# Rotary stage of a four-branch decoder trunk taken from PSUM with scaled tables, and a step per tile at the start of the last branch

## The chip, the cores and the metric

The program runs on one core of one Trainium2 chip. Its time is the device time of one execution in microseconds (us). Five engines run their own in-order queues: TensorE (PE, matmuls), VectorE (DVE), ScalarE (ACT), GpSimd (POOL) and SyncE (SP, which here issues DMAs). Matmul results land in PSUM, in banks of 128 x 512 float32 numbers, and are read from there by DVE or ACT.

## What is computed

The reference is a decoder trunk of two layers, 512 tokens, width 1024, in float32. Each layer runs four causal token mixers over one shared input projection, gates and adds them, and then a SwiGLU:

```python
for l in range(DEPTH):                       # DEPTH = 2
    h = rms_norm(x, ln1[l])
    u = h @ w_in
    fq, fk, fv, ff, gq, gk, gv, glr, gr, rq, rk, rv, rg, z, xbc, dt, gates = split_cols(u, IN_SPLITS)
    y_a = forgetting_attention(fq, fk, fv, ff + fox_bf, fox_qn, fox_kn)   # per-head RMS norm of q and k first
    o_b = gla_chunked(gq, gk, gv, log_a)
    o_c = retention_chunked(apply_rotary(rq, cos, sin), apply_rotary(rk, cos, sin), rv, log_gamma)
    o_d = ssd_chunked(...)
    merged = sum of sigmoid(gate_b) * (y_b @ w_up_b) over the four branches
    x = x + merged @ w_out
    x = x + swiglu(rms_norm(x, ln2[l]), w_ffn_in, w_ffn_out)

def apply_rotary(x, cos, sin):
    x1, x2 = x[..., :half], x[..., half:]    # half = 32 of a head's 64 channels
    return concatenate([x1 * cos - x2 * sin, x1 * sin + x2 * cos], axis=-1)
```

## The kernel before

Activations lie with the channels on the partitions and the 512 tokens along the free axis, so a tile of 128 x 512 holds two heads of 64 channels. Each float32 operand is split into a high and a low part in a reduced float32 type (`split` at L213 to L216: an ACT cast for the high part, a DVE subtraction for the low part), and a product is made as three matmuls, high by high, high by low and low by high (`mm3`), or as two (`mm2`) where one side is an exact constant.

**Weights** are streamed in slabs of 128 x 1024 (eight blocks of 128 x 128). For each slab SP issues a DMA into `wr`, ACT casts it to `wh` (L214), and DVE subtracts to `wl` (L215), two slabs ahead of their use.

**A projection tile** (`proj`) is eight k-blocks of three matmuls, 24 matmuls of 128 x 512 into one bank of the pool `mm` (four banks). Then a DVE instruction takes it out: L487 multiplies it with the norm's root `n1.r`, L1157 does the same for a gate tile, and L1171 multiplies the output of an up-projection (6 matmuls for a branch of 256 channels) with its gate. All else uses four banks of a second pool, `mx`. A bank is written again four tiles later, and not before the instruction that takes its old contents out.

**Order.** The four mixers are Python generators: `ssd`, `gla`, `ret` (retention) and `fox` (the forgetting attention). `drain(gen, PACE[i])` runs one to its next `yield w` and then emits projection and up-projection tiles from the list `fill` worth w times PACE[i] us (5.2 us for each projection tile); what is overdrawn is carried over. The scheduler of the framework then fixes the order on each engine at build time; at run time each engine takes its instructions strictly in that order.

**Names and lines that matter here.** `gate_quad` (L1148 on) makes a tile `g` of four gate tiles and applies one ACT sigmoid of 128 x 2048 when the fourth is there. ACT functions belong to sets of tables: Ln and Exp to one, Sigmoid to another, and `act` (L233, L238) issues an ACT_TABLE_LOAD where the set changes. In `ret()`, four tiles rq and rk (two each) are split, multiplied with the constant `perm` (L923, two matmuls of 128 x 512 for each tile, which exchange the halves of 32 channels with a sign), and put together as rq*cosT + (perm rq)*sinT by a DVE, a POOL and a DVE instruction (L928 to L930). In `fox()`, the four tiles fq and fk are normed: their squares are split and summed per head on PE with the constant `bones` (the bank named `mx`, from `t` and `cr`), ACT takes Ln and Exp of each (1/root), `newton` refines it with three DVE instructions (L371 reads the bank, L372, L373), and DVE L1036 scales the tile. Up to this change all of that comes before one `yield 2`, and `stack(0, 0)` before a `yield` of 1.

Of the kernel before, what the change touches and what calls it, by code (L numbers as in the profile page):

```python
# [13 lines left out]
AF = mybir.ActivationFunctionType  # L14
ALU = mybir.AluOpType
# [3 lines left out]
P = 128  # L19
S = 512  # L20
D = 1024
KD = D // P
# [10 lines left out]
C_RQ, C_RK, C_RV, C_RG = 1812, 2068, 2324, 2580  # L33
# [4 lines left out]
WARM = 11  # L38
TILE = 5.2
LAG = 1  # L40
PACE = (4.5, 5.0, 5.0, 7.5)
WIDE = 256 + 28
PARTS = (6, 6, 6, 4)
PLAIN = 2
# [11 lines left out]
def _const_parts():  # L56
    i = np.arange(P)
    same = (i[:, None] // 64) == (i[None, :] // 64)
    up = (i[:, None] <= i[None, :]).astype(np.float64)
    perm = np.zeros((P, P))  # L60
    for m in range(P):
        if m % 64 < 32:
            perm[m + 32, m] = -1.0
        else:
            perm[m - 32, m] = 1.0
    dret = np.zeros((P, NH, P))
    rel = i[None, :] - i[:, None]
    for h in range(NH):
        dret[:, h, :] = np.where(rel >= 0, np.exp(np.maximum(rel, 0) * LOGG[h]), 0.0) * 0.125
    qdec = np.zeros((P, 2, P))  # L70
    for j in range(2):
        for half in range(2):
            qdec[64 * half:64 * half + 64, j, :] = np.exp((i + 1.0) * LOGG[2 * j + half])[None, :]
    kdec = np.exp((P - 1.0 - i)[:, None] * LOGG[None, :]) * 0.125
    inv = (10000.0 ** (-np.arange(32) / 32.0))[i % 32][:, None]
    sgn = np.repeat(np.array([-1.0] * 4 + [1.0] * 8)[None, :], P, 0)
    one = np.ones((P, 1))
    exact = [
        ("uo", np.concatenate([up, np.ones((P, P))], 1)),
        ("lst", (i[:, None] > i[None, :]).astype(np.float64)),  # L80
        ("bones", same.astype(np.float64)),
        ("ubd", up * same),
        ("perm", perm),
        ("sel8", ((i[:, None] % 8 == np.arange(8)[None]) & (i[:, None] < 64)).astype(np.float64)),
        ("selc", ((i[:, None] % 32 // 4 == np.arange(8)[None]) & (i[:, None] < 64)).astype(np.float64)),
        ("sel4", ((i[:, None] % 4 == np.arange(4)[None]) & (i[:, None] % 32 < 16) & (i[:, None] < 64)).astype(np.float64)),
    ]
    return exact, [
        ("ident", np.eye(P)),
        ("dret", dret.reshape(P, -1)),  # L90
        ("qdec", qdec.reshape(P, -1)),
        ("kdec", kdec),
        ("inv", inv),
        ("sgn", sgn),
        ("blk8", (i[:, None] // 8 == np.arange(4)[None]).astype(np.float64)),
        ("blkc", np.where(i < 64, 1.0, -1.0)[:, None] * (i[:, None] % 4 == np.arange(4)[None])),
        ("blk4", (i[:, None] // 4 == np.arange(4)[None]).astype(np.float64)),
        ("eps", one * EPS),
        ("one", one),
        ("hpi", one * (math.pi / 2)),  # L100
    ]
# [33 lines left out]
def trunk(ctx: ExitStack, tc: tile.TileContext, keys, qkeys, xin, pos, wst, wsq, par, ext, cst, out):  # L135
    nc = tc.nc
    V, A, G, T = nc.vector, nc.scalar, nc.gpsimd, nc.tensor

    cp = ctx.enter_context(tc.tile_pool(name="cp", bufs=1))
    gap = [ctx.enter_context(tc.tile_pool(name="gap0", bufs=1))]  # L140
# [22 lines left out]

    def phase(**bufs):
        if not pools:
            for g, n in zip(gap, (32, 256)):
                if n:
                    pad(g, n)
        st = ExitStack()
        pad(st.enter_context(tc.tile_pool(name=nm("gap"), bufs=1)), 128 if "fp" in bufs else 64)  # L170
        for n, b in bufs.items():
            pools[n] = st.enter_context(tc.tile_pool(name=nm(n), bufs=b, reuse_waits="tile"))
        return st
# [4 lines left out]
    def TT(dtype=F32):  # L178
        return pools["tp"].tile([P, S], dtype, tag="t", name=nm("t"))

    def NT(dtype=F32):
        return np_.tile([P, S], dtype, tag="n", name=nm("n"))
# [7 lines left out]
    def MX():  # L190
        return px.tile([P, S], F32, tag="mx", name=nm("mx"))
# [16 lines left out]
    def mm2(o, l, r, start, stop):  # L208
        pairs = [(a, r) for a in l] if isinstance(l, tuple) else [(l, b) for b in r]
        for i, (a, b) in enumerate(pairs):  # L210
            mm(o, a, b, start and i == 0, stop and i == 1)
# [6 lines left out]
    def split_tile(t):  # L218
        return split(t, TT(F32R), TT(F32R))
# [9 lines left out]
    def act(out, in_, func, **kw):  # L229
        want = {AF.Ln: "natural_log_exp_and_others", AF.Exp: "natural_log_exp_and_others", AF.Silu: "silu_and_others", AF.Sin: "silu_and_others", AF.Sigmoid: "sigmoid_and_others"}.get(func)  # L230
        pre = None
        if want and want != seen["set"]:
            pre = A.preload_act_table_set(want)  # L233
            if seen["last"] is not None:
                order(pre, seen["last"])
            seen["set"] = want
            seen["pre"] = pre
        i = A.activation(out=out, in_=in_, func=func, **kw)  # L238
        if want:
            order(i, seen["pre"])  # L240
            seen["last"] = i
        return i
# [90 lines left out]
    def C(n):  # L333
        o, w = CONST_OFF[n]
        return cs[:, o:o + w]

    def R(n):
        o, w = EXACT_OFF[n]
        return cr[:, o:o + w]

    ident = C("ident")
    lst, bones, ubd, perm, uo = (R(n) for n in ("lst", "bones", "ubd", "perm", "uo"))
    sel8 = R("sel8").rearrange("p (g r) -> p r g", g=2)
    sel4, selc = R("sel4"), R("selc")
    U, ones = uo[:, :P], uo[:, P:2 * P]
# [6 lines left out]
    cosT = cp.tile([P, S], F32, name="cosT")  # L352
    sinT = cp.tile([P, S], F32, name="sinT")

    def rotary():
        ang = TT()
        V.tensor_copy(out=ang, in_=posi.pop())
        V.tensor_scalar(out=ang, in0=ang, scalar1=C("inv"), scalar2=None, op0=ALU.mult)
        n = TT()
        V.tensor_scalar(out=n, in0=ang, scalar1=1.0 / (2 * math.pi), scalar2=12582912.0, op0=ALU.mult, op1=ALU.add)  # L360
        V.tensor_scalar(out=n, in0=n, scalar1=-12582912.0, scalar2=None, op0=ALU.add)
        for c in _two_pi_parts():
            V.scalar_tensor_tensor(out=ang, in0=n, scalar=-c, in1=ang, op0=ALU.mult, op1=ALU.add)
        V.tensor_scalar(out=ang, in0=ang, scalar1=3.1415925, scalar2=-3.1415925, op0=ALU.min, op1=ALU.max)
        act(out=sinT, in_=ang, func=AF.Sin)
        act(out=n, in_=ang, func=AF.Abs)
        act(out=cosT, in_=n, func=AF.Sin, scale=-1.0, bias=hpi)

# [66 lines left out]
    def proj(name, l, c, src, nk):  # L435
        ps = MM()
        for k in range(nk):
            mm3(ps, block(name, l, k, c), src[k], k == 0, k == nk - 1)
        return ps

    def layer(l, n1, scope):
# [9 lines left out]
        fill = []  # L451
# [32 lines left out]
        def scaled(ps, scale=None):  # L484
            t = TT()
            if scale is None:
                V.tensor_tensor(out=t, in0=ps, in1=n1.r, op=ALU.mult)  # L487
            else:
                V.scalar_tensor_tensor(out=t, in0=ps, scalar=scale, in1=n1.r, op0=ALU.mult, op1=ALU.mult)
            return t  # L490
# [18 lines left out]
        def keep(dst, i, c, scale=None):  # L509
            def go():  # L510
                dst[i] = scaled(proj("w_in", l, c, n1, KD), scale)
            return TILE, go

        def tokmajor(dst, c, stacked=False):
# [77 lines left out]
        ps = MX()  # L592
# [321 lines left out]
        rq, rk, rv = [None] * 2, [None] * 2, []  # L914
        yc = [None] * 2

        def ret():
            pp = []
            sr = [split_tile(t) for t in rq + rk]
            yield 0.8  # L920
            for t in sr:
                ps = MX()
                mm2(ps, perm, t, True, True)  # L923
                pp.append(ps)
            yield
            for ps, t in zip(pp, rq + rk):
                u = TT()
                V.tensor_tensor(out=u, in0=ps, in1=sinT, op=ALU.mult)  # L928
                G.tensor_tensor(out=t, in0=t, in1=cosT, op=ALU.mult)
                V.tensor_tensor(out=t, in0=t, in1=u, op=ALU.add)  # L930
            yield
            qd = []
            for j in range(2):
                t = TT()
# [3 lines left out]
            for j in range(2):  # L938
# [6 lines left out]
                for half, ps in enumerate(pa):  # L945
                    t = TT()
# [4 lines left out]
            for j in range(2):  # L951
                ps = MX()
                for tb in range(NB):
                    T.transpose(ps[:, tb * P:(tb + 1) * P], rk[j][:, tb * P:(tb + 1) * P], ident)  # L954
                t = TT()
# [3 lines left out]
            ps = MX()  # L959
# [55 lines left out]
        def fox():  # L1015
# [8 lines left out]
            for q in fsq:  # L1024
                ps = MX()
# [3 lines left out]
            for ps in pn:  # L1029
                u = TT()  # L1030
                act(out=u, in_=ps, func=AF.Ln, scale=1.0 / 64, bias=eps)
                rs_.append(u)
            for i, u in enumerate(rs_):
                act(out=u, in_=u, func=AF.Exp, scale=-0.5)
                newton(u, pn[i], 64)
                V.scalar_tensor_tensor(out=qk[i], in0=qk[i], scalar=g8 if i < 2 else PR("fkn"), in1=u, op0=ALU.mult, op1=ALU.mult)  # L1036
            yield 2

            stk = {}

# [59 lines left out]
                    ya[hd // 2] = split_tile(t)  # L1100

            stack(0, 0)
            yield
            pend = []
            t = None
            step = 0
# [77 lines left out]

        fill += [keep(gq, j, C_GQ + P * j, 0.125) for j in range(2)] + [keep(gk, j, C_GK + P * j) for j in range(2)]
        fill += silus([C_GR, C_GR + P, C_RG, C_RG + P])
        fill += [keep(rq, j, C_RQ + P * j) for j in range(2)] + [keep(rk, j, C_RK + P * j) for j in range(2)]
        drain(ssd(), PACE[0])
        fill += tokmajor(rv, C_RV)
        fill += gate_quad(3, 0) + mix(gate_quad(3, 1), up_of(3, 0))  # L1190
# [17 lines left out]
        m = merged  # L1208
# [323 lines left out]
```

## Time and profile before

| | before |
|---|---|
| median of 3 runs | 1709.49 us (1709.37 to 1709.84) |
| the profiled execution's own time | 1709.5 us |
| its span in the profile | 1707.8 us |
| busy: DVE, ACT, POOL | 1215.3 us (71%), 863.5 us (51%), 216.8 us (13%) |

The span runs from the first to the last instruction that the profiler recorded; 1.7 us of the execution lie around it. The busy time of an engine is the sum over its instructions. Matmuls are pipelined: each one of 128 x 512 lasts 0.39 to 0.40 us in the records, while the next one begins about 0.23 us after it.

### The profile page before, as it was taken

To read this page: it belongs to the slowest core of one execution; us is meant where nothing else is said; L and a number is where in the kernel's file an instruction comes from. 1 tells how busy PE (TensorE), PEld (TensorE's weight loads), DVE (VectorE), ACT (ScalarE), POOL (GpSimd) and SP (SyncE) were. 2 spreads that over 40 slices of the span, in tenths; PEclk is the share of its full clock that TensorE was granted. 3 is DMA by queue.
4 is the path that set the end of the run, shared out by engine and by line. 5 is a ranking of instruction groups with operands and counts; after the bars stand their busy time and mean duration, and the time that the engine had idled before them with its cause. 6 is when DMAs were issued, how large, how long until landed. Compare 5 with 4: busy or idle time off the path is not lost.

```text
span 1707.8 us, 25188 instructions
## 1 busy us (share of the span) xinstructions
PE 1695.8 (99%) x10164; PEld 1475.3 (86%) x10164; DVE 1215.3 (71%) x1691; ACT 863.5 (51%) x1190; POOL 216.8 (13%) x221
## 2 busy tenths in 40 slices
PE   8999999999999999999999999999999999999998
PEld 7878888888888999998988788888888889999997
DVE  6867676768677677676777666767776677767666
ACT  5435543546347646464544354435554474655643
POOL 3021220022101010101020212201221010101010
PEclk9999999999999999999999999999999999999999
DMA  5322222222235657575333222222222365665753
GB/s 206 100 74 75 75 87 75 87 87 74 88 110 141 193 133 188 136 184 120 92 100 111 73 75 75 90 81 89 76 85 87 99 177 160 152 176 139 186 105 105
DMA packets 54693, 195.00 MB, mean 114 GB/s; under 512 B 6064, under 2 KB 6448, under 8 KB 54576
## 3 DMA queue, kind: packets, MB, share of 16 engines
q1 hardware_dynamic: 45072, 160.45, 29.9%
q0 software_dynamic: 8640, 31.46, 10.4%
q8 instruction: 79, 1.29, 0.3%
q10 hardware_dynamic: 864, 1.48, 0.2%
q14 instruction: 38, 0.31, 0.1%
HBM read 191.28 MB, written 2.10 MB: 113 GB/s over the span
## 4 chain that ended last, share of the span: by engine, by line
PE 96%; DVE 1%; ACT 1%; DMA 1%; issue 0%; ACTq 0%; DVEq 0%
PE mm L200 65%; PE mx L200 31%; PE mx L1082 1%; DMA x<-in_x_dram 0%; DMA t<-in_ext_dram 0%; ACT wh L214 0%; DVE wl L215 0%; PE mx L692 0%; DVE t L372 0%; ACT L233 0%; DVE t L836 0%; ACT g L238 0%; DVE t L1171 0%; PE mx L954 0%; PE mx L871 0%
## 5 line engine op out<-in xcount | busy, mean ns | idle before, releaser
L214 ACT CAST wh<-wr 128x1024 fp32r<-128x1024 f32 (+1 forms) x240 | 250.1, 1043 | 359.8 <-PE mm L200 207.5
L200 PE MATMUL mm<-xh,wh 128*128 128x512 f32 (+1 forms) x1184 | 428.4, 362 | 1.4 <-DVE t L1171 0.9
L200 PE MATMUL mm<-xh,wl 128*128 128x512 f32 (+1 forms) x1184 | 427.5, 361 | 0.0
L200 PE MATMUL mm<-xl,wh 128*128 128x512 f32 (+1 forms) x1184 | 427.5, 361 | 0.0
L215 DVE TENSOR_TENSOR wl<-wr,wh 128x1024 fp32r<-128x1024 f32 (+1 forms) x220 | 285.6, 1300 | 110.3 <-ACT wh L214 108.0
L200 PEld LDWEIGHTS mm<-xh,wh 128*128 128x128 f32 x1184 | 222.4, 188 | 36.3 <-DVE t L1171 1.8
L200 PEld LDWEIGHTS mm<-xl,wh 128*128 128x128 f32 x1184 | 222.4, 188 | 34.4 <-issue 1.5
L200 PEld LDWEIGHTS mm<-xh,wl 128*128 128x128 f32 x1184 | 222.5, 188 | 33.8 <-issue 0.6
L200 PE MATMUL mm<-t,wh 128*128 128x512 f32 x448 | 140.3, 392 | 0.0
L200 PE MATMUL mx<-xh,wh 128*128 128x256 f32 (+1 forms) x448 | 136.1, 311 | 3.1 <-ACT wh L214 3.1
L200 PE MATMUL mx<-xl,wh 128*128 128x256 f32 (+1 forms) x448 | 138.3, 309 | 0.0
L1290 POOL DMA_DIRECT2D wl<-in_wsq_dram x60 | 52.0, 867 | 517.4 <-ACT wl L1289 416.4
L200 PE MATMUL mx<-f,wh 128*128 128x512 f32 x352 | 108.2, 390 | 0.0
L200 PE MATMUL mm<-f,wh 128*128 128x512 f32 x352 | 105.9, 389 | 0.0
L200 PEld LDWEIGHTS mm<-t,wh 128*128 128x128 f32 x448 | 83.2, 188 | 17.3
L215 DVE TENSOR_TENSOR l<-rq,wh 128x1024 fp32r<-128x1024 f32 x60 | 73.2, 1220 | 33.0 <-ACT wh L214 18.6
L200 PEld LDWEIGHTS mx<-xh,wh 128*128 128x128 f32 x448 | 84.0, 188 | 9.3 <-ACT wh L214 4.2
L200 PE MATMUL mx<-xh,wl 128*128 128x256 f32 (+1 forms) x288 | 91.0, 327 | 0.0
L200 PEld LDWEIGHTS mx<-xl,wh 128*128 128x128 f32 x448 | 84.1, 188 | 5.1
L200 PE MATMUL mm<-t,wl 128*128 128x512 f32 x224 | 87.4, 390 | 0.0
L214 ACT CAST wh<-rq 128x1024 fp32r<-128x1024 f32 x60 | 63.0, 1049 | 43.8 <-PE mm L200 21.5
L200 PEld LDWEIGHTS mm<-f,wh 128*128 128x128 f32 x352 | 66.1, 188 | 13.5
(275 smaller groups left out, 3428.6 us busy)
## 6 DMA issues: line engine op xcount, KB each, us to landing
wr<-in_wst_dram SPq DMA_DIRECT2D x216, 512.0 KB, 3.5
rq<-in_wsq_dram SPq DMA_DIRECT2D x60, 512.0 KB, 5.6
wl<-in_wsq_dram POOLq DMA_DIRECT2D x60, 512.0 KB, 6.8
wr<-in_wsq_dram SPq DMA_DIRECT2D x20, 512.0 KB, 6.8
out_dram<-x SPq DMA_DIRECT2D x8, 256.0 KB, 2.0
x<-in_x_dram SPq DMA_DIRECT2D x3, 512.0 KB, 6.7
wr<-in_wst_dram SPq DMA_DIRECT2D x4, 256.0 KB, 5.6
x<-in_x_dram SPq DMA_DIRECT2D x2, 256.0 KB, 4.5
```

The costliest lines, as they stand in the source:

```text
L200: T.matmul(o, lhsT=l, rhs=r, start=start, stop=stop, skip_group_check=True)
L214: A.copy(out=hi, in_=src)
L215: V.tensor_tensor(out=lo, in0=src, in1=hi.bitcast(F32), op=ALU.subtract)
L1082: T.transpose(ps[:, W:W + P], zs[qb][:, kb * P:(kb + 1) * P], ident)
L1290: G.dma_start(out=lo, in_=wsq[j], accum_op=ALU.add)
```

## The change

The rotary stage no longer goes through PE. `turned` takes the place of `keep` for the four tiles rq and rk: when their projection is in its bank, four ACT copies of 32 partitions each write the halves exchanged into `u`, DVE multiplies the bank with cosT times the norm's root, `u` with sinT times the norm's root, and adds. The two tables are made once in each layer, and the sign is put into sinT (a per-partition factor of the Sin activation). The first three parts of `ret()` go, with their yields (0.8 + 1 + 1), and PACE[2] goes from 5.0 to 7.0, so that the remaining yields of `ret` ask for as much `fill` as before (49 us). In `fox()` the `yield 2` behind the norm becomes a `yield 0.4` behind each of its four tiles, and the `yield` behind the first `stack` becomes `yield 1.4`: 3.0 in both. The first padding of memory goes from 32 to 0, which with the constant `perm` gone moves the tiles behind the constants by 512 bytes.

```diff
-PACE = (4.5, 5.0, 5.0, 7.5)
+PACE = (4.5, 5.0, 7.0, 7.5)
...
-        ("perm", perm),
...
+        ("turn", np.where(i % 64 < 32, -1.0, 1.0)[:, None]),
...
-            for g, n in zip(gap, (32, 256)):
+            for g, n in zip(gap, (0, 256)):
...
-        act(out=sinT, in_=ang, func=AF.Sin)
+        act(out=sinT, in_=ang, func=AF.Sin, scale=C("turn"))
...
+        tables = []
+
+        def turned(dst, i, c):
+            def go():
+                if not tables:
+                    for e in (cosT, sinT):
+                        tables.append(NT())
+                        V.tensor_tensor(out=tables[-1], in0=e, in1=n1.r, op=ALU.mult)
+                ps = proj("w_in", l, c, n1, KD)
+                t, u = TT(), TT()
+                for a in range(0, P, 32):
+                    A.copy(out=u[a:a + 32], in_=ps[a ^ 32:(a ^ 32) + 32])
+                V.tensor_tensor(out=t, in0=ps, in1=tables[0], op=ALU.mult)
+                V.tensor_tensor(out=u, in0=u, in1=tables[1], op=ALU.mult)
+                V.tensor_tensor(out=t, in0=t, in1=u, op=ALU.add)
+                dst[i] = t
+            return TILE, go
...
         def ret():
-            pp = []
-            sr = [split_tile(t) for t in rq + rk]
-            yield 0.8
-            for t in sr:
-                ps = MX()
-                mm2(ps, perm, t, True, True)
-                pp.append(ps)
-            yield
-            for ps, t in zip(pp, rq + rk):
-                u = TT()
-                V.tensor_tensor(out=u, in0=ps, in1=sinT, op=ALU.mult)
-                G.tensor_tensor(out=t, in0=t, in1=cosT, op=ALU.mult)
-                V.tensor_tensor(out=t, in0=t, in1=u, op=ALU.add)
-            yield
...
                 V.scalar_tensor_tensor(out=qk[i], in0=qk[i], scalar=g8 if i < 2 else PR("fkn"), in1=u, op0=ALU.mult, op1=ALU.mult)
-            yield 2
+                yield 0.4
...
             stack(0, 0)
-            yield
+            yield 1.4
...
-        fill += [keep(rq, j, C_RQ + P * j) for j in range(2)] + [keep(rk, j, C_RK + P * j) for j in range(2)]
+        fill += [turned(rq, j, C_RQ + P * j) for j in range(2)] + [turned(rk, j, C_RK + P * j) for j in range(2)]
```

Over both layers PE loses 16 matmuls of 128 x 512 and keeps all others; DVE loses 8 each of L215 (128 x 512), L487, L928 and L930 and gains 28 (4 tables, 24 in `turned`); ACT loses 8 casts and gains 32 copies of 32 x 512; POOL loses the 8 of L929; SP issues the same DMAs in the same order. ACT's table loads keep their number.

**ACT at the norm of fox, first layer.** Before, with `t_2815`, `t_2817`, `t_2819` and `t_2821` the roots of the four tiles, `mx_...` the banks with their sums, `g_2611` a tile of four gates and `wh_...` the casts of slabs:

```order
L238 ACTIVATE t_2815<-mx_2803,cs 128x512
L238 ACTIVATE t_2817<-mx_2806,cs 128x512
L238 ACTIVATE t_2815<-t_2815 128x512
L238 ACTIVATE t_2817<-t_2817 128x512
L238 ACTIVATE t_2819<-mx_2809,cs 128x512
L238 ACTIVATE t_2819<-t_2819 128x512
L238 ACTIVATE t_2821<-mx_2812,cs 128x512
L238 ACTIVATE t_2821<-t_2821 128x512
L233 ACT_TABLE_LOAD
L238 ACTIVATE g_2611<-g_2611 128x2048
L214 CAST wh_3000<-wr_2998 128x1024
L233 ACT_TABLE_LOAD
```

And with the change (the four roots are `t_2802`, `t_2804`, `t_2806` and `t_2808`, the gates `g_2604`; the line numbers are those of the changed file, L232 for L238, L227 for L233 and L208 for L214):

```order
L232 ACTIVATE t_2802<-mx_2790,cs 128x512
L232 ACTIVATE t_2804<-mx_2793,cs 128x512
L232 ACTIVATE t_2802<-t_2802 128x512
L232 ACTIVATE t_2804<-t_2804 128x512
L227 ACT_TABLE_LOAD
L232 ACTIVATE g_2604<-g_2604 128x2048
L227 ACT_TABLE_LOAD
L232 ACTIVATE t_2806<-mx_2796,cs 128x512
L208 CAST wh_2988<-wr_2986 128x1024
L232 ACTIVATE t_2808<-mx_2799,cs 128x512
L232 ACTIVATE t_2806<-t_2806 128x512
L232 ACTIVATE t_2808<-t_2808 128x512
```

The first two roots are unchanged; the load of the sigmoid's tables, the sigmoid and the load back now stand ahead of the third and the fourth root, and so does the cast `wh_2988`, which stood behind the sigmoid before.

**DVE at the same place.** Before, with L371 to L373 the steps of `newton`, L1171 (from `mm_2847` and `mm_2902`) and L1157 (from `mm_2918`) the instructions that take banks of projections out:

```order
L371 SCALAR_TENSOR_TENSOR t_2836<-mx_2809,t_2819 128x512
L372 SCALAR_TENSOR_TENSOR t_2824<-t_2824,t_2815 128x512
L372 SCALAR_TENSOR_TENSOR t_2830<-t_2830,t_2817 128x512
L371 SCALAR_TENSOR_TENSOR t_2842<-mx_2812,t_2821 128x512
L1171 TENSOR_TENSOR t_2866<-mm_2847,g_1901 128x512
L1171 TENSOR_TENSOR t_2915<-mm_2902,g_1901 128x512
L372 SCALAR_TENSOR_TENSOR t_2836<-t_2836,t_2819 128x512
L373 SCALAR_TENSOR_TENSOR t_2815<-t_2824,t_2815 128x512
L373 SCALAR_TENSOR_TENSOR t_2817<-t_2830,t_2817 128x512
L372 SCALAR_TENSOR_TENSOR t_2842<-t_2842,t_2821 128x512
L1157 TENSOR_TENSOR g_2917<-mm_2918,n_323 128x512
L215 TENSOR_TENSOR wl_3001<-wr_2998,wh_3000 128x1024
```

With the change (L365 to L367 for `newton`, L1034 for L1036, L1169 for L1171, L1155 for L1157, L209 for the subtraction that makes `wl`, L1043 and L1019 small steps of `stack` and of the next layer's constant):

```order
L209 TENSOR_TENSOR wl_2989<-wr_2986,wh_2988 128x1024
L1034 SCALAR_TENSOR_TENSOR t_2303<-t_2303,g_2788,t_2802 128x512
L365 SCALAR_TENSOR_TENSOR t_2879<-mx_2796,t_2806 128x512
L1034 SCALAR_TENSOR_TENSOR t_2336<-t_2336,g_2788,t_2804 128x512
L365 SCALAR_TENSOR_TENSOR t_2885<-mx_2799,t_2808 128x512
L1169 TENSOR_TENSOR t_2903<-mm_2890,g_1932 128x512
L209 TENSOR_TENSOR wl_3040<-wr_3037,wh_3039 128x1024
L366 SCALAR_TENSOR_TENSOR t_2879<-t_2879,t_2806 128x512
L1043 TENSOR_TENSOR t_2905<-t_2303,t_2905 64x512
L1019 TENSOR_SCALAR g_10747<-pr 128x1
L366 SCALAR_TENSOR_TENSOR t_2885<-t_2885,t_2808 128x512
L1155 TENSOR_TENSOR g_2918<-mm_2919,n_322 128x512
```

Of the two L1171 of the first listing, the counterpart of the first (it takes `mm_2816` out) now stands above these rows, behind a single L365. That of the second (`mm_2890`) stands behind `wl_2989`, which needs the cast `wh_2988`, and behind the L365 of the last two roots. The instruction that takes `mm_2919` out stands further down, behind a second slab `wl_3040`.

**ACT where rq and rk are projected, first layer.** Before, behind the Silu group of `ssd` (`t_1253` was its last):

```order
L233 ACT_TABLE_LOAD
L214 CAST wh_1428<-wr_1426 128x1024
L238 ACTIVATE t_1368<-t_1074 128x512
L238 ACTIVATE t_1370<-t_1075 128x512
L214 CAST t_1373<-t_1368 128x512
L238 ACTIVATE t_1377<-t_1076 128x512
L238 ACTIVATE t_1379<-t_1077 128x512
L214 CAST wh_1514<-wr_1512 128x1024
```

With the change:

```order
L227 ACT_TABLE_LOAD
L519 COPY t_1314<-mm_1282 32x512 x4
L208 CAST wh_1452<-wr_1450 128x1024
L519 COPY t_1377<-mm_1345 32x512 x4
L232 ACTIVATE t_1385<-t_1073 128x512
L232 ACTIVATE t_1387<-t_1074 128x512
L208 CAST t_1390<-t_1385 128x512
L208 CAST wh_1545<-wr_1543 128x1024
```

Four copies stand where each of the four tiles comes out of its bank (two of the four are seen here), between the casts of slabs and the chain of `ssd`'s norm, whose order among themselves is kept.

More of the change, by code (lines that the diff above doesn't have):

```diff
@@ L59, in _const_parts @@
     up = (i[:, None] <= i[None, :]).astype(np.float64)
[L60 to L65, printed above, removed]
     dret = np.zeros((P, NH, P))
@@ L341, in trunk @@
     ident = C("ident")
-    lst, bones, ubd, perm, uo = (R(n) for n in ("lst", "bones", "ubd", "perm", "uo"))
+    lst, bones, ubd, uo = (R(n) for n in ("lst", "bones", "ubd", "uo"))
     sel8 = R("sel8").rearrange("p (g r) -> p r g", g=2)
```

## Prediction, made before the changed kernel was run

> **What bounds the kernel now.** I read the page first: the busy shares, the clock, and the chain of work that ended last.
>
> ```profile
> PE 1695.8 (99%) x10164; PEld 1475.3 (86%) x10164; DVE 1215.3 (71%) x1691; ACT 863.5 (51%) x1190; POOL 216.8 (13%) x221
> ...
> PEclk9999999999999999999999999999999999999999
> ...
> PE 96%; DVE 1%; ACT 1%; DMA 1%; issue 0%; ACTq 0%; DVEq 0%
> ```
>
> PE is busy for 99% of the span, the last chain is 96% PE, and the clock granted to it is full in every slice. So the time is PE's queue plus the little that PE waits. Next comes PE's own view of waits, where each row is what PE waited for, the sum, how often, and the longest.
>
> ```profile
> PE mx L200 <- ACT wh L214: 3.1, 3, 1.7
> PE mm L200 <- POOL t L328: 1.4, 1, 1.4
> PE mx L200 <- DVE t L215: 1.2, 2, 0.7
> PE mm L200 <- DVE t L1171: 0.9, 2, 0.5
> PE mm L200 <- DVE t L489: 0.5, 1, 0.5
> ```
>
> That is 7.1 us in the whole run. The first two rows and the last belong to the start and to other stages. The third and fourth are in fox, one wait in each layer, in the stretch that the change reorders. Three questions follow: how much shorter does PE's queue get, which of these waits go, and which new ones come. DVE, ACT and POOL matter only where PE waits for them.
>
> **The matmuls that go.** The timeline of PE shows what one costs (start, duration):
>
> ```profile
> 222.36 0.40 PE L200 MATMUL mx<-t,cr 128*128 128x512 f32 x1
> 222.59 0.39 PE L200 MATMUL mm<-t,wh 128*128 128x512 f32 x1
> 222.82 0.40 PE L200 MATMUL mm<-t,wl 128*128 128x512 f32 x1
> ```
>
> The records overlap; what the queue pays is the distance of two starts, 0.23 us. Eight matmuls with `perm` go in each layer: 16 x 0.23 = **3.7 us off**. They lie among projections, so nothing waits in their place. What is left of PE's queue is the same set of matmuls in a slightly different order; starts after a short matmul differ from starts after a long one by tenths, and I take nothing for that, with 1 us to either side.
>
> The other engines' share of the old rotary stage (L928 to L930 and eight splits) was hidden under PE's 99%; its end gives nothing. The DMAs of SP keep their order and their number, and what is loaded stays the same.
>
> **The new work beside the projections of rq and rk.** The trace has no copy of 32 x 512 out of PSUM. The nearest rows are a copy of 64 x 512 out of PSUM and a cast of 32 x 512 out of SBUF (ns, minimum, median, maximum), and the window holds the four projections in the first layer (us, then the busy time of PE, PEld, DVE, ACT, POOL):
>
> ```profile
> L1097 ACT COPY t<-mx x8: 582/584/586, 382.3 to 1302.5; 64x512 f32<-64x512 f32 x8
> L614 ACT CAST t<-t x6: 614/621/622, 101.5 to 1135.2; 32x512 fp32r<-32x512 f32 x6
> 142.00:167.00 25.00, 25.00 (x174) 21.18 (x173) 19.36 (x27) 15.28 (x23) 6.53 (x5) 1.00 0.26 72
> ```
>
> So a copy costs 0.58 to 0.62 us, or a little less behind another; I take 0.58. In 25 us ACT has 25 - 15.3 = 9.7 us free, and 16 x 0.58 = 9.3 us are added; DVE has 5.6 us free, and eight more instructions of 0.6 us (three in place of one, for four tiles) add 4.8. Both just fit. The banks come free later by the copies' 2.3 us, while a bank is asked for again only three tiles (some 16 us) later; and the next casts for which PE waits, those of `ssd`'s norm, have some 4 us to spare when I put the new instructions into the queue by hand. I cost the stage at nothing (a gain is excluded, since PE doesn't wait there now). Its cover is those 4 us; what it costs without them is the third rival.
>
> **The old waits in fox that go.** From PE's timeline, in both layers, the wait behind L1171 and the one behind the split L215:
>
> ```profile
> 326.71 0.40 PE L200 MATMUL mx<-t,cr 128*128 128x512 f32 x1
> 327.56 0.50 PE L200 MATMUL mm<-xh,wh 128*128 128x512 f32 x1 [0.45 <-DVE t L1171]
> ...
> 1173.79 0.50 PE L200 MATMUL mm<-xh,wh 128*128 128x512 f32 x1 [0.45 <-DVE t L1171]
> ...
> 363.33 0.56 PE L200 MATMUL mx<-t,t 128*128 128x256 f32 x3 [0.53 <-DVE t L215]
> ...
> 1209.67 0.56 PE L200 MATMUL mx<-t,t 128*128 128x256 f32 x3 [0.66 <-DVE t L215]
> ```
>
> The first costs 327.56 - 326.71 - 0.23 = 0.62 us, and it goes: the instruction for which PE waited stands further up with the change, behind one L365 rather than three L371 and two L372. The second costs 0.53 and 0.66 us beside the refill of PE, some 0.1 us (the first matmul after a wait lasts 0.50 rather than 0.39). With the smaller steps at the start of fox, its softmax chain is spread otherwise, and in the listings the split no longer stands right ahead of PE's need. Together 2 x 0.62 + 0.53 + 0.66 + some refill = **2.7 us off**; between 1.2 (the second stays) and 2.9.
>
> **The new wait in fox.** Here I find the cost of the change. ACT before (start, duration):
>
> ```profile
> 319.35 1.26 ACT L238 ACTIVATE t<-mx,cs 128x512 f32<-128x512 f32 x2
> 320.50 1.15 ACT L238 ACTIVATE t<-t 128x512 f32<-128x512 f32 x2
> 323.03 0.69 ACT L238 ACTIVATE t<-mx,cs 128x512 f32<-128x512 f32 x1 [1.39 <-PE mx L200]
> ...
> 325.79 1.28 ACT L233 ACT_TABLE_LOAD   x1
> 327.08 1.92 ACT L238 ACTIVATE g<-g 128x2048 f32<-128x2048 f32 x1
> 328.90 1.04 ACT L214 CAST wh<-wr 128x1024 fp32r<-128x1024 f32 x1
> 329.96 1.28 ACT L233 ACT_TABLE_LOAD   x1
> ```
>
> Four roots first, then load, sigmoid and load. With the change load, sigmoid and load, 1.28 + 1.92 + 1.28 = 4.5 us, stand between the second root and the third, and the cast of a slab stands behind the third Ln. I put this on a clock that is 0 when PE starts the second matmul of the second norm sum. The chain of ACT: slab cast to 0.8, a small cast, Ln and Exp twice to 3.7; load, sigmoid, load to 8.2; Ln to 8.9, of which the cast overlaps 0.1; its end is at 9.9; Ln, Exp, Exp to 11.6. The durations of DVE are in these rows:
>
> ```profile
> 319.73 1.22 DVE L215 TENSOR_TENSOR wl<-wr,wh 128x1024 fp32r<-128x1024 f32 x1
> ...
> 326.23 0.68 DVE L371 SCALAR_TENSOR_TENSOR t<-mx,t 128x512 f32<-128x512 f32 x1
> 326.83 1.28 DVE L1171 TENSOR_TENSOR t<-mm,g 128x512 f32<-128x512 f32 x2
> ...
> 332.76 1.40 DVE L1036 SCALAR_TENSOR_TENSOR t<-t,g,t 128x512 f32<-128x512 f32 x2
> ```
>
> In a row one of 512 columns costs 0.6 us (the next starts before it ends), L1036 0.66, a slab 1.13. DVE is done with the first two roots at 7.5 and then stands at the slab's subtraction, whose cast ends at 9.9: all behind it waits. Then slab, L1036, L371, L1036, L371 (1.13 + 0.66 + 0.6 + 0.66 + 0.6) to 13.5, and the L1171 that frees a bank ends at 14.1. PE asks for that bank 60 matmuls after 0, at 60 x 0.228 = 13.7: a **wait of 0.5**. The bank after it is asked for six matmuls later, at 14.2 + 1.4 = 15.6. Ahead of the instruction that frees it stand a slab, two L372, a step of 64 x 512 and a tiny one (1.1 + 0.6 + 0.6 + 0.6 + 0.1): it ends at 17.9, a **wait of 2.3**. PE has fallen back by 2.8 us then, and the following needs (24 and 30 matmuls on) are met with time to spare. The order is the same in both layers: **5.6 us on**. What is uncertain is where DVE and ACT stand against PE at 0: an error of 1 us there moves each layer's wait by up to 1 us. At best it is nothing (DVE's 2.4 us at the slab are not spent); at worst the whole 4.5 us of ACT less the 0.5 us that PE would have had are seen, 4.0 in each layer.
>
> A rule of the Trainium skill speaks against such an order: "ScalarE: Activation LUTs", under "What ACT_TABLE_LOAD costs", counts a drain of 1380 ns with each load of 1283 ns. The rows agree with the load alone: 325.79 + 1.28 = 327.07, and the sigmoid starts at 327.08. By the page the two loads would take 2.8 us more in each layer.
>
> **The sum.** The rows come from an execution of 1709.5 us (span 1707.8 and 1.7 around it), which is the median too. 1709.5 - 3.7 - 2.7 + 5.6 = **1708.7 us**. I call it the same: a measurement of this kernel can tell about 0.2%, 3.4 us, from no change.
>
> **The rivals.**
>
> First, the new wait is small. For it speaks that my clock is set by hand from six instructions ahead of it, and that a backlog of 2.4 us on DVE decides it. If DVE comes to the slab earlier by a cast that ACT slips ahead, or if PE comes later, little of it is left. Against it: the in-order queues leave ACT's 4.5 us where they are. The time is then 1709.5 - 3.7 - 2.7 = 1703.1, and up to 1706 with less than half of the wait left. Faster; 0.38.
>
> Second, the old wait at the split stays beside the new one, or the chain of `gla`'s states, which now has up-projections mixed into its matmuls, makes PE wait for some tenths: 1708.7 + 1.5 = 1710.2, still the same. It is part of the 0.53 for the forecast.
>
> Third, slower: the stage of rq and rk. Its ACT queue is full to 9.3 of 9.7 us. If a copy that writes other partitions than it reads costs more than 0.58 us, 16 of them fall behind by 16 times the difference, and beyond the 4 us to spare PE waits for the casts behind them. That decides from 0.58 + 4 / 16 = 0.83 us on; at 1.05 us (the slab cast's 1.04) the loss is 16 x 0.47 - 4 = 3.5 us in a layer, so 1708.7 + 7 = 1715.7. Against it: all rows of ACT with 512 columns lie between 0.58 and 0.69 us. 0.06.
>
> Fourth, also slower: each table switch holds ACT for longer than its load when its neighbours depend on it. With 1.4 us more at each of the two loads in the new place, DVE's slab comes 2.8 us later, and PE's wait grows by that in both layers: 1708.7 + 5.6 = 1714.3. It needs what the rows at 325.79 and 327.08 exclude there. The page named above would give this. 0.03.
>
> **How the numbers follow.** Forecast 0.53 for within 0.2%; faster 0.38 by the first rival; slower 0.09 by the third and fourth. The range goes down to 1702.5 (the first rival, less some tenths for the order of the matmuls) and up to 1711.5 (the forecast with 1 us on for the order and the second rival); the forecast's own is 1706.1 to 1711.5.
>
> **What would show it.** In the profile after, 48 matmuls with `cr` and `t` rather than 64. In the waits of PE two rows for L1169 and L1155 of some 0.5 and 2.3 us in each layer, near the third root of fox; on ACT there load, sigmoid, load ahead of the third Ln, and DVE idle for about 2.4 us with the cast of a slab named as its releaser. No wait of PE in the stage of rq and rk, copies of about 0.58 us. I am wrong if PE waits there, if DVE doesn't stand still ahead of the slab, or if PE's waits in the whole run, which would sum to 7.1 - 2.1 + 5.6 = 10.6 us, sum to less than about 8.

## The result: slower, and the profile after

| | before | with the change |
|---|---|---|
| median | 1709.49 us (1709.29 to 1710.82, 5 runs) | 1718.72 us (1718.36 to 1720.61, 5 runs) |
| ratio to before, 95% interval | | 1.0055 [1.0043, 1.0067] |
| span of the profiled execution | 1707.8 us | 1717.0 us |

The change costs 9.2 us, where 0.8 us less was forecast. The page of the changed kernel begins like that of before: PE is the bound and the last chain is PE's.

```profile
PE 1702.3 (99%) x10148; PEld 1475.0 (86%) x10148; DVE 1202.4 (70%) x1687; ACT 875.4 (51%) x1214; POOL 206.1 (12%) x213
...
PE 97%; DVE 1%; ACT 1%; issue 0%; DMA 0%; DVEq 0%; ACTq 0%
```

PE is busy for 6.5 us longer with 16 matmuls less, and its waits, in its own view, grew by only 2.8 us (from 7.1 to 9.9):

```profile
PE mm L194 <- DVE g L1155: 4.9, 3, 2.2
PE mx L194 <- ACT wh L208: 2.6, 3, 1.1
PE mm L194 <- POOL t L322: 1.4, 1, 1.4
PE mx L194 <- DVE t L209: 0.6, 1, 0.6
PE mm L194 <- DVE t L1169: 0.4, 2, 0.2
```

So most of the loss is time in which PE runs and gets less done. To find it I laid the two traces beside each other at the first matmul of each weight slab (the slabs come in the same order in both) and took how far the changed kernel lags behind: -0.3 us ahead of gla, +3.0 behind the retention of the first layer, +6.0 behind its fox, +5.7 up to the second layer's gla, +5.9 behind its retention, +9.1 behind its fox, +9.2 at the end. With the 1.8 us in each layer that the removed matmuls give, gla and retention lost 5.1 and 2.0 us, and fox 3.0 and 3.2.

**The states of gla.** PE's timeline in the first layer (start, duration, engine, line, form, count of records; a float32 matmul has two records), before and then after:

```profile
211.07 1.92 PE L200 MATMUL mx<-t,sbd 64*64 64x64 f32 x56
212.91 0.73 PE L200 MATMUL mm<-t,wh 128*128 128x512 f32 x2
```

```profile
210.53 0.45 PE L194 MATMUL mx<-t,sbd 64*64 64x64 f32 x8
210.91 0.73 PE L194 MATMUL mm<-t,wh 128*128 128x512 f32 x2
211.57 0.44 PE L194 MATMUL mx<-t,sbd 64*64 64x64 f32 x4
211.95 0.50 PE L194 MATMUL mm<-t,wl 128*128 128x512 f32 x1
212.38 0.44 PE L194 MATMUL mx<-t,sbd 64*64 64x64 f32 x4
212.75 0.73 PE L194 MATMUL mm<-t,wh 128*128 128x512 f32 x2
213.41 0.33 PE L194 MATMUL mx<-t,sbd 64*64 64x64 f32 x2
213.67 0.50 PE L194 MATMUL mm<-t,wl 128*128 128x512 f32 x1
214.10 0.33 PE L194 MATMUL mx<-t,sbd 64*64 64x64 f32 x2
...
217.52 0.45 PE L194 MATMUL mx<-t,sbd 64*64 64x64 f32 x6
217.90 0.50 PE L194 MATMUL mm<-t,wh 128*128 128x512 f32 x1
```

The 56 records took 212.91 - 211.07 = 1.84 us in one run. Now ten up-projection matmuls stand between them, in nine runs from 210.53 to 217.90; less 10 x 0.227 us for these, the states take 5.1 us. No wait is shown. A matmul between two runs holds PE's queue for 0.43 us (213.67 to 214.10) rather than 0.23, and the two records behind it for 0.25 us. That is +3.3 us in the first layer; by the same count the second layer, with three runs, goes from 1.8 to 2.6 us and loses 0.9.

**The scores of the retention.** Before and after, first layer:

```profile
259.54 2.06 PE L200 MATMUL mx<-t,t 64*128 64x128 f32 x32
261.53 0.50 PE L200 MATMUL mm<-xh,wh 128*128 128x512 f32 x1
```

```profile
235.67 1.16 PE L194 MATMUL mx<-t,t 64*128 64x128 f32 x8
236.76 0.50 PE L194 MATMUL mm<-t,wl 128*128 128x512 f32 x1
...
237.65 1.16 PE L194 MATMUL mx<-t,t 64*128 64x128 f32 x8
238.74 0.50 PE L194 MATMUL mm<-xh,wl 128*128 128x512 f32 x1
...
243.95 1.49 PE L194 MATMUL mx<-t,t 64*128 64x128 f32 x16
```

These matmuls use one half of the array's rows. Before, the two halves took turns: 32 records in 1.99 us, 62 ns each. Now, in the built order, eight of one half come in a row, then others, and then eight of the other half: 1.09 us for eight, 136 ns each with the switch at either end. Within such a row the records start 112 ns apart; where the halves take turns, two start 7 ns apart and the next two 112 ns after them. Counted from the start of the matmul ahead of each, and without waits, the matmuls of this form (gla's own scores and these) take 1.4 and 1.1 us more in the two layers.

**Fox.** The two waits of the forecast are there:

```profile
339.63 0.49 PE L194 MATMUL mm<-xh,wh 128*128 128x512 f32 x1 [2.17 <-DVE g L1155]
...
340.66 0.43 PE L194 MATMUL mm<-xl,wh 128*128 128x512 f32 x1
340.90 0.63 PE L194 MATMUL mm<-xh,wl 128*128 128x512 f32 x1
341.32 0.63 PE L194 MATMUL mm<-xh,wh 128*128 128x512 f32 x1
...
343.88 0.58 PE L194 MATMUL mm<-xh,wh 128*128 128x512 f32 x1
344.30 0.40 PE L194 MATMUL mm<-xl,wh 128*128 128x512 f32 x1
```

Behind the wait of 2.17 us eight matmuls start 0.43 us apart, for 3.4 us, and the view of windows (length, busy PE, PEld, DVE, ACT, POOL, then the granted clock) shows why:

```profile
340.00:345.00 5.00, 5.00 (x17) 3.91 (x16) 4.47 (x9) 2.77 (x4) 0.84 (x1) 0.66 0.00 0
```

The clock granted to TensorE was halved there: 0.66 on average is half of it for 3.4 of the 5 us. That costs 8 x 0.2 = 1.6 us. In the second layer a wait of 2.11 us had no such tail, but one old wait stayed (0.65 us on L209) and a new one of 0.66 came (L1155).

In sum, against before: -3.6 (matmuls) + 4.1 (states) + 2.5 (scores) + 6.2 (fox) = +9.2 us. The sum is good to some tenths: it leaves 0.5 us of what gla and the retention lost unnamed, and 0.6 us that the change gains ahead of gla and between the layers about cancels that.

### The profile page after: what moved, and what is told of

Read it like the earlier page. It is cut to its first block, busy times and chain, and to the rows that moved or that the text cites. A ratio compares the mean times of both kernels' runs of the same rounds, so it can differ in the third digit from the quotient of the medians.

```text
span 1717.0 us, 25141 instructions
## 1 busy us (share of the span) xinstructions
PE 1702.3 (99%) x10148; PEld 1475.0 (86%) x10148; DVE 1202.4 (70%) x1687; ACT 875.4 (51%) x1214; POOL 206.1 (12%) x213
## 4 chain that ended last, share of the span: by engine, by line
PE 97%; DVE 1%; ACT 1%; issue 0%; DMA 0%; DVEq 0%; ACTq 0%
PE mm L194 66%; PE mx L194 31%; PE mx L1080 0%; DVE wl L209 0%; DMA x<-in_x_dram 0%; ACT wh L208 0%; PE mx L704 0%; ACT n L232 0%; DVE t L366 0%; ACT xh L232 0%; DVE t L1169 0%; DVE g L1155 0%; PE mx L952 0%; PE mx L883 0%; DVE n L404 0%
## 5 line engine op out<-in xcount | busy, mean ns | idle before, releaser
L208 ACT CAST wh<-wr 128x1024 fp32r<-128x1024 f32 (+1 forms) x240 | 249.7, 1043 | 378.2 <-PE mm L194 211.7
L209 DVE TENSOR_TENSOR wl<-wr,wh 128x1024 fp32r<-128x1024 f32 (+1 forms) x220 | 279.5, 1272 | 106.7 <-ACT wh L208 102.4
L209 DVE TENSOR_TENSOR l<-rq,wh 128x1024 fp32r<-128x1024 f32 x60 | 73.2, 1221 | 32.6 <-ACT wh L208 18.6
L208 ACT CAST wh<-rq 128x1024 fp32r<-128x1024 f32 x60 | 63.0, 1050 | 43.7 <-PE mm L194 21.5
```

Source lines behind the costliest of these rows:

```text
L208: A.copy(out=hi, in_=src)
L209: V.tensor_tensor(out=lo, in0=src, in1=hi.bitcast(F32), op=ALU.subtract)
```

## Experiments

Each is an edit of the changed kernel, but for the second. Ratios are to the kernel before, measured beside each, with their 95% intervals.

**1. Fox's old steps.**

```diff
-                yield 0.4
+            yield 2
...
-            yield 1.4
+            yield
```

> The changed kernel with fox's old steps (yield 2 behind the norm, yield 1 behind the first stack), all else as changed. My theory: the two waits in fox and the halved clock behind the first of them go, the two old waits come back: 1718.7 - 6.2 = about 1712.5 us, mean granted clock 1.000, no wait of PE on L1155 in fox, and the states of gla and the scores of retention as slow as with the change. Rival (the delay comes from the rotary stage's copies and lands in fox only by chance): the wait stays somewhere, 1717 to 1719.

Measured: 1720.34 us, ratio 1.0060 [1.0045, 1.0075]. The theory fell: fox waits longer, 3.3 us in each layer, both times with a halved clock behind it (some 8 matmuls).

```profile
329.66 0.40 PE L194 MATMUL mx<-t,cr 128*128 128x512 f32 x1
333.40 0.50 PE L194 MATMUL mm<-xh,wh 128*128 128x512 f32 x1 [3.34 <-DVE t L1169]
```

Here all four roots precede the sigmoid again, and yet DVE stands at a slab's subtraction ahead of the instruction that frees the bank. Fox's new steps are not what brings the wait.

**2. Fox's new steps alone, on the kernel before.**

```diff
-            yield 2
+                yield 0.4
...
-            yield
+            yield 1.4
```

> The kernel before with only fox's new steps (0.4 behind each tile, 1.4 behind the stack). My theory: the sigmoid's loads land between the roots here too, so PE waits some 0.4 and 2.3 us in each layer, with half the clock behind it where it falls so: 1709.5 + 6 = about 1715.5 us, at least 1712.5 without the clock's part. Rival (the wait needs the rotary stage's new order as well): within 0.2% of 1709.5.

Measured: 1710.01 us, ratio 1.0001 [0.9992, 1.0011]. The rival holds. PE's view of waits:

```profile
PE mm L200 <- DVE g L1157: 2.8, 2, 1.4
PE mx L200 <- ACT wh L214: 2.2, 2, 2.0
```

The sigmoid stands between the roots here too, but each wait is 1.4 us, they replace the old ones (2.1 us together), and no halved clock follows them.

**3. The states of gla in one sequence.**

```diff
-            for j, po in enumerate(pos_):
-                for n in range(1, 8):
+            prev = None
+            for n in range(7, 0, -1):
+                for j, po in enumerate(pos_):
...
-                        mm(po[hs, cs_], sbd[hs, n - 1, j, hs], qd[j][hs, cs_], False, n == 7)
+                        i = mm(po[hs, cs_], sbd[hs, n - 1, j, hs], qd[j][hs, cs_], False, n == 1)
+                        if prev is not None:
+                            order(i, prev)
+                        prev = i
```

> The changed kernel; only the 28 matmuls of 64 x 64 with gla's states are tied into one sequence, from the last state to the first, so that the scheduler leaves the up-projections ahead of or behind them (two runs of them in each layer, not nine and three). My theory: the switches between full-array and 64 x 64 matmuls cost 3.3 us in the first layer and 0.9 in the second, so 1718.7 - 3.5 = about 1715.2 us, if PE doesn't come to wait for the last state. Rival (the 64 x 64 matmuls are slow because of the states' arrival, not of the order): a wait of PE on DVE takes their place and the time stays at 1718 to 1719.

Measured: 1719.37 us, ratio 1.0057 [1.0041, 1.0074]: no gain. The states did become cheap (2.2 us in each layer, from 5.1 and 2.6), and no wait took their place. But the scheduler then put all scores of the retention by halves, four pieces in each layer, and these cost 0.9 and 1.2 us more. The 1.2 us that this count leaves of the gain are within the spread of its runs (1718.1 to 1720.9). Here the first fox wait (2.18 us) had a full clock behind it and the second (2.12 us) a halved one.

**4. The scores in the order of their code.**

```diff
+                prev = None
                 for tb in range(NB):
...
-                        mm(pa[half][:, ts], rk[j][hs, ts], rq[j][hs, ts], True, True)
+                        i = mm(pa[half][:, ts], rk[j][hs, ts], rq[j][hs, ts], True, True)
+                        if prev is not None:
+                            order(i, prev)
+                        prev = i
```

> The changed kernel; only the retention's 32 score matmuls in each layer are tied into the order of their code, so that the two row halves of the array alternate again. My theory: neighbours on the same half take 112 ns each, neighbours on different halves 112 ns for the two, so 1.4 and 1.1 us go: 1718.7 - 2.5 = about 1716.2 us. Rival (they are slow because their operands now come from other instructions and addresses): 1718.7, and still 112 ns for each.

Measured: 1718.09 us, ratio 1.0048 [1.0033, 1.0063], which can't be told from the change. In the trace the halves alternate, at 1.16 us for 14 records rather than for 8:

```profile
236.00 0.49 PE L194 MATMUL mx<-t,t 64*128 64x128 f32 x2
...
238.68 1.16 PE L194 MATMUL mx<-t,t 64*128 64x128 f32 x14
```

So it is the order and not the operands that makes them slow. But projections still stand in each group, and by the count only 0.5 and 0.7 us of the 2.5 come back.

**5 and 6. The steps of the retention.** The change takes three yields out of `ret()` and raises the pace of the rest. Put back, they are empty:

```diff
-PACE = (4.5, 5.0, 7.0, 7.5)
+PACE = (4.5, 5.0, 5.0, 7.5)
...
         def ret():
+            yield 0.8
+            yield
+            yield
             qd = []
```

Number 5 has fox's old steps as well, so that only the arithmetic, and the padding, of the change is left; number 6 has fox's new ones.

> The changed kernel with the steps of retention (0.8, 1 and 1, now empty, at a pace of 5.0) and of fox as before: only the arithmetic of the rotary stage is changed. My theory: the scores alternate again, since fill stands between gla's end and them (-2.5 us against the change), the states stay cut up as with the change, and fox, which meets fill at the place of before, waits some 1.2 us in each layer as before rather than 3.3: 1709.85 - 3.7 + 4.1 = about 1710.3 us. Rival (fox's wait comes from the rotary stage): 2 to 3 us of wait in each layer, 1714 to 1716.

> The changed kernel with the steps of retention as before and fox's new ones. My theory: as the kernel before with fox's new steps alone there, waits of 1.4 us on L1157's counterpart in each layer and no halved clock, scores alternating, states cut up: about 1710.5 us. Rival as in the run before: 1715 and more.

Measured: 1710.35 us, ratio 1.0003 [0.9993, 1.0012], and 1711.76 us, 1.0011 [1.0001, 1.0020]. Number 5 against number 1 is the one edit above, steps and pace together, and it is worth 10.0 us; number 6 against the change is the same edit, worth 7.0 us. In number 5 the waits in fox are those of before, and the scores take 4.5 us in each layer by the count above (4.7 before, 6.0 and 5.7 with the change):

```profile
PE mx L194 <- DVE t L209: 1.2, 2, 0.7
PE mm L194 <- DVE t L1172: 0.9, 2, 0.4
```

Number 6 has the shape of number 2, with three waits on the gate tiles rather than two (the third is 0.7 us, later in the first layer's fox):

```profile
PE mm L194 <- DVE g L1158: 3.5, 3, 1.4
```

The states stay cut up in both (5.1 and 2.6 us). That part comes with the rotary stage itself: the built order of the states is the same with the old padding.

**7 and 8. The states tied as well.** The edit of number 3 on top of number 6 (number 7) and of number 5 (number 8).

> The run before, and the states of gla tied together as in the third experiment. My theory: their switches go too, which is 3.1 us over both layers: about 1707.4 us. Rival (PE comes to wait for the last state, or the scores lose their order again): no gain against the run before.

> Retention's and fox's steps as before, and the states tied together: the arithmetic of the change in the order of before as far as it goes. My theory: the 16 matmuls' 3.7 us show up at last: about 1707 us, faster than the kernel before by 0.15%. Rival (the new instructions beside the projections cost what the matmuls saved): 1709.5 or more.

Measured: 1709.07 us, ratio 0.9997 [0.9987, 1.0006], and 1707.62 us, 0.9986 [0.9977, 0.9996]. Tying the states gives 2.7 us each time, and now the scores keep their order. Number 7 is 1.7 us above its forecast, which started from the 1710.5 us expected of number 6: that one came out 1.3 us higher, and its 3.5 us of waits on gate tiles stay. Number 8 is the first version faster than before. In PE's timeline the states of gla are two runs again, with one up-projection matmul between them and the others ahead or behind:

```profile
218.07 0.44 PE L194 MATMUL mx<-t,sbd 64*64 64x64 f32 x6
218.44 0.51 PE L194 MATMUL mm<-xh,wl 128*128 128x512 f32 x1
218.88 1.73 PE L194 MATMUL mx<-t,sbd 64*64 64x64 f32 x50
220.53 0.50 PE L194 MATMUL mm<-xh,wh 128*128 128x512 f32 x1
```

**9. Number 8 again.**

> The kernel of the run before (arithmetic of the change, steps of before, states tied) once more, with more rounds. If its gain is real: a ratio of about 0.9986 whose interval stays under 1. If it was chance: an interval that holds 1.

Measured: 1707.49 us, ratio 0.9986 [0.9977, 0.9995]. The gain of 2.3 us is real, though small.

**10. The changed kernel again, for its clock.**

> The changed kernel once more, for its clock only. If the halving behind a wait of 2.2 us follows from the wait's length, it is there in the first layer again and not in the second; if it depends on where the wait falls, it can be in either, both or none. Time about 1718 to 1721 us.

Measured in one run: 1717.42 us. The waits of 2.17 and 2.12 us are there in both layers, and neither has a halved clock behind it:

```profile
335.00:345.00 10.00, 7.61 (x32) 5.64 (x32) 9.43 (x16) 3.46 (x6) 0.76 (x1) 1.00 0.21 71
1184.00:1194.00 10.00, 7.88 (x35) 6.17 (x34) 9.85 (x14) 2.78 (x4) 1.46 (x1) 1.00 0.17 54
```

So the halving behind a wait of this length differs from one execution of the same program to the next.

## Why the prediction was wrong, point by point

- **The matmuls that go (3.7 us off): right.** 64 such matmuls became 48, and number 8, in which nearly all else is as before, is faster by 2.3 us. Its states still take 2.2 us in each layer rather than 1.8, and gla and the retention together are 1.0 and 1.3 us shorter than before, where the matmuls alone would give 1.8 each.
- **"A slightly different order ... I take nothing for that, with 1 us to either side": this is the step that failed.** By the count it measured +6.6 us: 4.1 for states that switch between 64 x 64 and the full array nine and three times rather than once, 2.5 for scores whose halves no longer take turns. The order was known before the run. I read it for waits and priced matmuls as if their neighbours didn't matter, although the trace of before shows runs of both forms without a wait in them, and their ends (0.73 us for two matmuls behind the states, 0.62 us elsewhere). In time, experiments 7 and 8 show 2.7 us of the states' part; the scores' part rests on the count, since experiment 4 gave back too little to be measured.
- **The new wait in fox: right in place, mechanism and size**, 0.2 and 2.2 us where 0.5 and 2.3 were forecast, and DVE stands still ahead of the slab for 2.3 us where 2.4 were counted (the rows below, one of each layer). Even so, fox as a whole cost 6.2 us where the new waits less the old ones were to cost 2.9. Two things were missing. The halved clock behind it was not in the sum (1.6 us in the profiled run of the result). And I read the wait as a result of fox's new steps, while experiments 1, 2 and 5 show that it belongs to the removal of the retention's steps: with these gone fox waits 2.2 or 3.3 us, with these back 0.4 or 1.4, whichever steps fox has. The pace went back with the steps each time; which of the two decides was not tried.

```profile
331.40 1.23 DVE L209 TENSOR_TENSOR wl<-wr,wh 128x1024 fp32r<-128x1024 f32 x1 [2.26 <-ACT wh L208]
...
1180.49 1.23 DVE L209 TENSOR_TENSOR wl<-wr,wh 128x1024 fp32r<-128x1024 f32 x1 [2.27 <-ACT wh L208]
```

- **The old waits that go (2.7 us): half right.** The first went in both layers, the second only in the first layer; in the second 0.65 us stayed and 0.66 came.
- **The rotary stage beside the projections (nothing): right.** The copies took 579 ns, PE waits for nothing between 140 and 300 us, and ACT is at 22.1 of 25 us in the window for which 9.3 added to 15.3 were counted (all 16 copies lie in it, and five other instructions no longer do).

```profile
L519 ACT COPY t<-mm x32: 575/579/583, 147.2 to 1018.2; 32x512 f32<-32x512 f32 x32
...
142.00:167.00 25.00, 25.00 (x175) 20.92 (x174) 17.38 (x24) 22.06 (x34) 6.04 (x5) 1.00 0.26 73
```

- **The rivals.** None had the true cause. The first, a small wait, fell: the waits are 2.17 and 2.11 us. The third and fourth, which would have made it slower, did not happen: on ACT load, sigmoid and load follow each other without a pause (325.22, 326.51 and 328.45, and the next Ln at 329.74). The second named the chain of gla's states with the up-projections mixed in, but priced it as a wait of some tenths; it costs no wait, and 4.1 us.

Why these orders come out is in part argued. With the three steps gone, the retention's scores come directly behind gla's end. The two banks that the halves need would then come free at different times, which would separate the halves; the runs show that the steps, with their pace, decide it, not that the banks are the reason. And why the rotary stage makes the scheduler cut gla's states up was not tried.

## What to carry to other kernels

- On a kernel that is 99% matmul, compare the order on PE itself before and after an edit, and count where matmuls of another form or another part of the array cut into a run of their kind: such a change has no row among the waits, and here it was worth more than the edit.
- An empty yield can matter more than the work that it once separated: the three steps of `ret()`, with their pace, were worth 10.0 us without anything in them (7.0 us with fox's new steps). Take work out first, and the steps around it in an experiment of their own.
- A wait of PE of some 2 us can have a price beyond its length, since a halved clock may follow (1.6 us in the profiled run of the result).

## What the runs showed of the hardware

- **Switching.** A matmul of 128 x 512 between two runs of 64 x 64 holds the queue for 0.43 us rather than 0.23, and the return to 64 x 64 costs a further tenth or two: some 0.4 us for each excursion. The Trainium skill, "TensorEngine Tiling (Array Packing)", "Key Properties", says that a change of the tiling mode drains the engine; it gives no time, and these rows do.
- **Row halves.** Of float32 matmuls on one half of the rows, 8 records on the same half hold the queue for 1.09 us (235.67 to 236.76 in the change), and 14 whose halves alternate for 1.08 us (238.68 to 239.76 in experiment 4): one record every 112 ns against two, apart from the switch at either end.
- **The clock.** Of eight waits of 2.11 to 2.18 us in four profiles (the change twice, experiments 3 and 4), three were followed by some 3.4 us at half the clock and five by none; the two of 3.34 us both were; the six of 1.4 us in experiments 2, 6 and 7 never were. At the start of the program, where PE waits for the cast of the first slab, it is alike: behind 1.8 to 2.0 us (experiments 2, 5, 6 and 10) half the clock follows, behind 1.0 to 1.7 us (the other eight profiles) it doesn't. The rows are experiment 2, with a wait of 2.04 us, and before, with 1.73. The Trainium skill, "TensorE: Matmul & The Clock Gate", Part 1, lets the clock fall after an idle window of about 3.4 us that runs freely. Here 1.8 us of idle time were at times enough, and that the same program shows it in one run and not in another agrees with a window that is not tied to the program.

```profile
8.00:11.00 3.00, 3.00 (x9) 2.33 (x8) 1.85 (x4) 2.97 (x6) 0.00 (x0) 0.51 1.02 401
...
8.00:11.00 3.00, 3.00 (x14) 2.30 (x13) 2.05 (x4) 2.96 (x5) 0.34 (x1) 1.00 1.03 407
```
